# Masked token products of a chunked RWKV-7 mixer as 64x64 blocks on the array's quarters, and a pair's inversion ahead of the next pair's operands

## The chip, the core and the metric

One program on one core of a Trainium2 chip. The metric is the device time of one execution in microseconds; lower is better. The engines named below are TensorE (PE, whose weight loads are listed apart as PEld), VectorE (DVE), ScalarE (ACT), GpSimd (POOL) and SyncE (SP, which here only issues DMAs, in the order in which they stand in its queue). Each engine takes its instructions in program order and waits on semaphores.

## The reference, cut to what matters

One decoder layer on 512 tokens with a model width of 2048: a modulated RMS norm, one wide projection, two token mixers side by side (RWKV-7 and a gated width-3 convolution), a gated merge, an output projection and a residual. All arithmetic is fp32. The part that the change touches is the recurrence of the RWKV-7 mixer, 16 heads of size 64:

```
def step(S, inp):
    r_t, w_t, k_t, v_t, kk_t, b_t = inp
    sa = jnp.einsum('bhvk,bhk->bhv', S, -kk_t)
    S = (S * w_t[:, :, None, :] + sa[..., None] * b_t[:, :, None, :]
         + v_t[..., None] * k_t[:, :, None, :])
    y_t = jnp.einsum('bhvk,bhk->bhv', S, r_t)
    return S, y_t
```

## The kernel before

The recurrence is computed in chunks of C = 64 tokens, NC = 8 chunks, for a pair of heads at a time (two heads of 64 fill the 128 partitions), so there are NP = 8 pairs. In a chunk every product of one token's B or K row with another token's A or R row is needed (A is minus the normalised key, R the receptance, B and K the two things written to the state, each scaled by its decay). They are the tiles `GB` and `GK`, one 128 x 128 square per chunk: rows are the tokens of B (or K) of both heads, columns are the tokens of A and R.

The kernel has three stages. The first makes the normalised input as two fp32r halves (`hH`, `hL`) and opens some of the projection. The second, which the change is in, is `dense()`: 81 column tiles of the projection, each 48 matmuls of 128x128 weights and 512 moving columns (`ps_c`; half of each weight tile is split off by ACT and POOL as `wH_c` and `wL_c`), and between those matmuls the small work of the mixers. The third multiplies by the gates, `p_a`, `p_b` and `w_out`.

The order of the second stage on every engine is written by a planner in the kernel itself. Generators, the entries of the list `sides`, describe each piece of small work as steps with due times; `run(engine, cost, ...)` issues one instruction and books its cost on that engine, `take(tag, ...)` takes a PSUM bank when its last reader is due to be done, and `spend(t)` advances the clock `now` by PE's cost. At each step of the clock the entries of `sides` are asked in their order, and then one `dense()` matmul is issued. For each pair there are three of these pieces:

- `prepare` ("ops"): the operand tiles `AR` (A and R) and `BK` (B and K). In a square of `BK` each head stands in its own 64 partitions and its own 64 columns, and the other two quarters are zero; so the product of a square with `AR` over all 128 partitions keeps the heads apart.
- `invert` ("inv"): the products. For B and then for K, and for four chunks at a time, it takes one bank of tag `pg` (there are two), issues four fp32 matmuls 128x128 by 128 columns (L760), and lets DVE multiply the bank by a triangular 0/1 mask into `GG`. Then GB's 32x32 diagonal blocks go by DMA through DRAM (`s1`) into `M`, 31 steps of two DVE instructions (`invt`, `Xg`) invert them, copies and two more passes through DRAM (`s2`, `s3`) bring them to `XB` and `M`, and two sets of sixteen 32x32 matmuls (`pw`, `py`, L834) fill in the rest.
- `chunks`: transposes of BK and V, and then a chain over the eight chunks, in which PE, ACT and DVE take turns (`p1`, `p2`, `UB`, `SB`), group norm, and the transposes back by 64x64 matmuls on two of the array's quarters (tile `y`, L956).

An fp32 matmul leaves two records in the trace: `pg` has 128 matmuls and 256 records.

Of the kernel before, what the change touches and what calls it, by code (L numbers as in the profile page):

```python
# [8 lines left out]
F32 = mybir.dt.float32  # L9
F32R = mybir.dt.float32r  # L10
I32 = mybir.dt.int32
AF = mybir.ActivationFunctionType
ALU = mybir.AluOpType
# [3 lines left out]
P = 128  # L17
T = 512
# [4 lines left out]
NH = 2  # L23
HS = 64
C = 64
NC = T // C
HB = C // 2
# [8 lines left out]
HOP, SURE, SOON, SUM = 0.2, 0.6, 1.2, 0.35  # L36
# [40 lines left out]
def trunk(ctx: ExitStack, tc: tile.TileContext, xT_d, x_d, prm_d, adan_d, ada1_d, ada2_d, rows_d, w_d, lora_d, pa_d, pb_d,  # L77
          wo_d, out_d):
    nc = tc.nc
    V, A, G, TE, S = nc.vector, nc.scalar, nc.gpsimd, nc.tensor, nc.sync  # L80

    cst = ctx.enter_context(tc.tile_pool(name="cst", bufs=1))
# [9 lines left out]
    def bank(tag, name, n=T):  # L92

        return psp[tag].tile([P, T], F32, tag=tag, bufs=BANKS[tag], name=name)[:, 0:n]
# [21 lines left out]
    hsumr = cst.tile([P, P], F32R, name="hsumr")  # L116
    V.tensor_copy(hsumr, hsum)

    gmask = cst.tile([P, P], F32, name="gmask")
    G.memset(gmask, 1.0)  # L120
    for r0 in (0, C):
        for c0, op in ((r0, ALU.is_gt), (C - r0, ALU.is_ge)):
            G.affine_select(gmask[r0:r0 + C, c0:c0 + C], gmask[r0:r0 + C, c0:c0 + C], [[1, C]], op, 0.0, base=0,
                            channel_multiplier=-1)
    omu = cst.tile([P, 25], F32, name="omu")
    V.tensor_scalar(omu, pc("mu", 0, 25), -1.0, 1.0, ALU.mult, ALU.add)
    hw0 = cst.tile([P, 16], F32, name="hw0")
# [58 lines left out]
    with tc.tile_pool(name="ap", bufs=1) as ap, tc.tile_pool(name="psa", bufs=1, space=PSUM) as psa:  # L186
# [114 lines left out]
        for k in range(KT):  # L301
            g = 32 * (k % 4)
            TE.matmul(psc[g:g + 32, :], csb[:, k, :], adan[k // 8][:, k % 8, :], start=(k < 4), stop=(k >= KT - 4),
                      tile_position=(0, g))
# [29 lines left out]
        now = COST["begin"]  # L334
        clk = dict(dve=now + 1.4, act=now + 0.7, pool=now + 1.5, dma=now + 16.5)
        ready, lands, cut = {0: now}, {1: now + 2.0, 2: now + 9.8, 3: now + 16.5}, {b: now + 0.4 * b for b in range(3)}
# [5 lines left out]
        done, opened, units, at = 0, [], [], {}  # L342
# [63 lines left out]
        while units or opened:  # L406
# [3 lines left out]
            if u is None and units and len(opened) < NOPEN:  # L410
                b, t, k0, n = units[0]
# [8 lines left out]
            b, t, ps, k0, n, i = u  # L420
# [20 lines left out]
    with tc.tile_pool(name="rp", bufs=1) as rp, tc.manual_schedule(engines=ALL):  # L441


        now = 0.0
# [3 lines left out]
        def spend(t):  # L448
            nonlocal now
            now += t  # L450

        def run(eng, cost, f, *args, **kw):

            two = eng in ("POOL", "DVE2")
            e = eng[:3] if eng == "DVE2" else eng
            while busy[e] > now + SOON:
                yield busy[e] - SOON
            f(*args, **kw)  # L458
            t = max(now, busy[e])
            if two:  # L460
                while port and port[0][1] <= now:
                    port.pop(0)
                for b, c in port:
                    if b < t + cost and t < c:
                        t = c
                port.append((t, t + cost))
                port.sort()
            busy[e] = t + cost
            return busy[e] + HOP
# [9 lines left out]
        books = {tag: [[0.0] for _ in range(n)] for tag, n in BANKS.items()}  # L479

        def take(tag, name, n=T):
            while books[tag][0][0] is None or books[tag][0][0] > now:
                yield now + 0.25 if books[tag][0][0] is None else books[tag][0][0]
            books[tag].pop(0)
            book = [None]
            books[tag].append(book)
            return bank(tag, name, n), book

        def four(ps):
            return ps.rearrange("p (a b) -> p a b", a=4)  # L490
# [4 lines left out]
        def c3(t):  # L495
            return t.rearrange("p (c t) -> p c t", c=NC)
# [17 lines left out]
        halves = (slice(0, HS), slice(HS, P))  # L514


        hold, rkv, ops = {}, [dict() for _ in range(NP)], [dict() for _ in range(NP)]
# [141 lines left out]
        def prepare(j, got, out):  # L659
            n = f"_{j}"  # L660
# [3 lines left out]
            for i, b in enumerate(halves):  # L664
                o = halves[1 - i]
                t = yield from run("ACT", 0.3, A.activation, raw[o, 1, i].bitcast(F32R), raw[o, 0, i], AF.Copy)
# [3 lines left out]
                t = yield from run("POOL", 0.46, G.tensor_tensor, wa[o, i], raw[o, 0, i], raw[o, 1, i], ALU.subtract)  # L670
            yield t + SURE
            psw, book = yield from take("sm", "ps_w" + n)
# [5 lines left out]
            psa, book = yield from take("sm", "ps_a" + n)  # L678
            lowrank(psa, wa[:, 1], 1)
            yield from run("DVE", 0.55, V.tensor_scalar, lw, lw, -0.5 * DECAY, -0.5 * DECAY, ALU.mult, ALU.add)  # L680
            cum3 = c3(lw)
            for t0 in range(0, T, T // 4):
                t = yield from run("DVE2", 0.42, V.tensor_tensor_scan, lw[:, t0:t0 + T // 4],
                                   keep.rearrange("p c t -> p (c t)"), lw[:, t0:t0 + T // 4], 0.0, ALU.mult, ALU.add)
# [12 lines left out]
            kr = got["k"]  # L697
# [6 lines left out]
            psk, book = yield from take("sm", "ps_k" + n)  # L704
# [17 lines left out]
            AR = rp.tile([P, NC, P], F32, tag="AR", bufs=2, name="AR" + n)  # L722
            BK = BKs[j % 2]
            yield from run("DVE2", 0.7, V.tensor_tensor, a, kk, a, ALU.mult)
            for h, b in enumerate(halves):
                o = halves[1 - h]
                yield from run("DVE2", 0.7, V.scalar_tensor_tensor, AR[b, :, b], c3(kk)[b], -1.0, dec[b, :, 0:C], ALU.mult,
                               ALU.mult)
                yield from run("DVE2", 0.7, V.tensor_tensor, BK[b, :, 0, b], c3(a)[b], cum3[b], ALU.mult)
                yield from run("DVE2", 0.7, V.tensor_tensor, AR[b, :, o], c3(rr)[b], dec[b, :, 1:C + 1], ALU.mult)  # L730
                t = yield from run("DVE2", 0.7, V.tensor_tensor, BK[b, :, 1, b], c3(kr)[b], cum3[b], ALU.mult)

            u = yield from run("DVE2", 0.7, V.scalar_tensor_tensor, kr, rr, pc("rk", j), kr, ALU.mult, ALU.mult)
            out.update(AR=AR, end=end, vpad=got["vpad"], made=t)
# [7 lines left out]
            psb, book = yield from take("sm", "ps_b" + n)  # L742
# [6 lines left out]
        def invert(j, AR, out, made, **_):  # L749

            n = f"_{j}"
            yield made + SURE

            GB, GK = (yield from room_of("GG")) if j % 2 else (GG[:, 0], GG[:, 1])
            BK = BKs[j % 2]
            for i, g in enumerate((GB, GK)):
                for c0 in (0, 4):
                    pg, book = yield from take("pg", f"pg{n}_{c0}_{i}")
                    for k in range(4):
                        TE.matmul(four(pg)[:, k, :], BK[:, c0 + k, i, :], AR[:, c0 + k, :], start=True, stop=True)  # L760
                    spend(0.9)
                    yield now + SUM
                    book[0] = yield from run("DVE", 0.7, V.tensor_tensor, g[:, c0:c0 + 4, :], four(pg),
                                             gmask.unsqueeze(1).to_broadcast([P, 4, P]), ALU.mult)
                if not i:
                    ready = book[0]

            while at["z"] < j or not at["zeros"]:
                yield now + 0.3
# [52 lines left out]

            def lower(name, left, right, out):

                ps, books = [], []
                for h in range(NH):
                    p, book = yield from take("pg", f"{name}{h}{n}", NC * HB)
                    ps.append(p.rearrange("p (c t) -> p c t", c=NC))
                    books.append(book)
                for c in range(NC):  # L830
                    for h in range(NH):
                        l, r = left(h, c), right(h, c)
                        row = h * C + (HB if name == "py" else 0)
                        TE.matmul(ps[h][blk[h][1], c, :], l, r, start=True, stop=True,  # L834
                                  tile_position=(row, h * C + HB))
                spend(0.7)
                yield now + SUM
                for h in range(NH):
                    t = yield from run("ACT", 0.38, A.activation, out(h), ps[h][blk[h][1]], AF.Copy)
                    books[h][0] = t  # L840
                return t

            yield SURE + (yield from lower("pw", lambda h, c: GB[blk[h][0], c, blk[h][1]],
# [5 lines left out]
        def chunks(j, AR, GB, GK, bon, end, vpad, solved, **_):  # L849

            n = f"_{j}"
# [4 lines left out]
            BK = BKs[j % 2]  # L856
# [17 lines left out]
            for c0, m in ((0, 4), (4, 4), (8, 1)):  # L874
                pv, book = yield from take("pg", f"pv{n}_{c0}")
                pv = four(pv)
                for k in range(m):
                    TE.transpose(pv[:, k, :], vpad[:, (c0 + k) * C:(c0 + k + 2) * C], ident)
                spend(0.11 * m)
                yield now + SUM  # L880
                for h, b in enumerate(halves):

                    k0, k1 = max(c0 + h - 1, 0), min(c0 + m + h - 1, NC)
                    if k0 < k1:
                        w0 = k0 + 1 - h - c0
                        t = yield from run("ACT", 0.38, A.activation, VB[b, k0:k1, b], pv[b, w0:w0 + k1 - k0, b], AF.Copy)
                book[0] = t
            turned.add(j)
            yield max(turned_b, solved) + SURE
# [199 lines left out]
        def side(name, behind, make):  # L1089
            for j in range(NP):  # L1090
                while not behind(j):
                    yield now + 0.3
                yield from make(j)
                at[name] = j + 1
# [8 lines left out]
        for i in range(NFULL):  # L1103
# [2 lines left out]
        sides = [[g, 0.0] for g in (  # L1106
            high(), low(), loader(), uses(soon), uses(due),
            side("chunks", lambda j: "solved" in ops[j] and "bon" in ops[j], lambda j: chunks(j, **ops[j])),
            side("ops", paced, lambda j: prepare(j, rkv[j], ops[j])),
            side("inv", lambda j: at["made"] > j, lambda j: invert(j, out=ops[j], **ops[j])),  # L1110
            zeros())]
        stream, idle = dense(), 0.0
        while stream or any(sd[0] for sd in sides[5:]) or due or soon:
# [298 lines left out]
```

## Time and profile before

| what | value |
|---|---|
| median of 3 runs | 1621.15 us (1621.15 to 1621.32) |
| the profiled execution: time, span of its core | 1618.96 us, 1617.0 us |
| mean granted TensorE clock | 0.996 |
| PE, DVE, POOL, ACT busy | 99%, 58%, 50%, 40% of the span |
| stage 2 | about 188 to 1236 us |
| first `pg` matmul of the first and of the last pair | 261.7 us and 1047.0 us |
| DMA | 235.72 MB, mean 146 GB/s |

PE's busy time counts the whole way of a matmul through the array, and matmuls overlap, so what one of them costs is read as the distance from its start to the next start and not as its duration (`ps_c` lasts 396 ns in the trace, and the starts are nearer together). Idle time of the other engines costs nothing as long as PE has no wait for them.

### The profile page before, as it was taken

To read this page: it belongs to the slowest core of one execution; us is meant where nothing else is said; L and a number is where in the kernel's file an instruction comes from. 1 tells how busy PE (TensorE), PEld (TensorE's weight loads), DVE (VectorE), ACT (ScalarE), POOL (GpSimd) and SP (SyncE) were. 2 spreads that over 40 slices of the span, in tenths; PEclk is the share of its full clock that TensorE was granted. 3 is DMA by queue.
4 is the path that set the end of the run, shared out by engine and by line. 5 is a ranking of instruction groups with operands and counts; after the bars stand their busy time and mean duration, and the time that the engine had idled before them with its cause. 6 is when DMAs were issued, how large, how long until landed. Compare 5 with 4: busy or idle time off the path is not lost.

```text
span 1617.0 us, 23221 instructions
## 1 busy us (share of the span) xinstructions
PE 1593.0 (99%) x8194; PEld 1323.1 (82%) x8194; DVE 931.4 (58%) x1643; ACT 641.2 (40%) x1305; POOL 812.7 (50%) x648
## 2 busy tenths in 40 slices
PE   7999999999999999999999999999999999999997
PEld 6788878888888888888888888888888888888886
DVE  6997397764978827816869359353111354453404
ACT  5554442324545235335443353344433223223421
POOL 2799574553435534544445435434344446765421
PEclk9999999999999999999999999999999999999999
DMA  9986334333322343333333433434353786765714
GB/s 365 366 333 212 102 117 112 97 111 87 101 85 85 100 118 88 102 112 106 96 99 99 115 105 94 127 101 116 92 166 117 242 266 192 202 206 171 240 36 150
DMA packets 139172, 235.72 MB, mean 146 GB/s; under 512 B 34864, under 2 KB 43696, under 8 KB 135216
## 3 DMA queue, kind: packets, MB, share of 16 engines
q1 hardware_dynamic: 138912, 234.15, 47.0%
q8 instruction: 65, 1.06, 0.3%
q14 instruction: 51, 0.42, 0.1%
q10 hardware_dynamic: 144, 0.09, 0.0%
HBM read 214.78 MB, written 19.14 MB: 145 GB/s over the span
## 4 chain that ended last, share of the span: by engine, by line
PE 95%; DVE 3%; ACT 1%; issue 0%; DMA 0%; POOL 0%; POOLq 0%; ACTq 0%
PE ps_c L1071 53%; PE fps L162 3%; PE fps L161 3%; PE fps L160 3%; PE po L161 3%; PE po L160 3%; PE po L162 3%; PE py_a L162 2%; PE py_b L161 2%; PE py_a L160 2%; PE py_b L160 2%; PE py_b L162 2%; PE py_a L161 2%; PE pg L760 2%; PE pl L162 1%; PE pl L161 1%
## 5 line engine op out<-in xcount | busy, mean ns | idle before, releaser
L458 POOL TENSOR_TENSOR wL_c<-raw_c,wH_c 128x512 fp32r<-128x512 f32 x324 | 440.9, 1362 | 538.2 <-ACT wH_c L458 508.4
L1071 PE MATMUL ps_c<-hH,wL_c 128*128 128x512 f32 x1296 | 513.3, 396 | 0.7 <-POOL wL_c L458 0.7
L1071 PE MATMUL ps_c<-hH,wH_c 128*128 128x512 f32 x1296 | 513.6, 396 | 0.0
L1071 PE MATMUL ps_c<-hL,wH_c 128*128 128x512 f32 x1296 | 512.0, 395 | 0.0
L458 ACT ACTIVATE wH_c<-raw_c 128x512 fp32r<-128x512 f32 x324 | 204.1, 630 | 423.7 <-PE ps_c L1071 270.0
L1071 PEld LDWEIGHTS ps_c<-hH,wL_c 128*128 128x128 f32 x1296 | 243.8, 188 | 48.6 <-POOL wL_c L458 1.1
L1071 PEld LDWEIGHTS ps_c<-hL,wH_c 128*128 128x128 f32 x1296 | 243.8, 188 | 47.0
L1071 PEld LDWEIGHTS ps_c<-hH,wH_c 128*128 128x128 f32 x1296 | 243.8, 188 | 46.8
L149 POOL TENSOR_TENSOR fL<-fraw,fH 128x512 fp32r<-128x512 f32 x56 | 79.8, 1434 | 45.6 <-ACT fH L148 45.4
L458 DVE TENSOR_TENSOR Xg<-Xg,invt 128x60 f32<-128x60 f32 (+24 forms) x248 | 92.3, 372 | 7.9
L149 POOL TENSOR_TENSOR oL<-wo,oH 128x512 fp32r<-128x512 f32 x48 | 65.8, 1379 | 61.0 <-ACT oH L148 58.3
L160 PE MATMUL fps<-hH,fH 128*128 128x512 f32 x224 | 88.8, 396 | 3.5 <-ACT hH L269 3.5
L458 DVE TENSOR_TENSOR invt<-M,Xg 128x60 f32<-128x60 f32 (+24 forms) x248 | 87.1, 351 | 7.9
L161 PE MATMUL fps<-hL,fH 128*128 128x512 f32 x224 | 88.8, 396 | 2.2 <-DVE hL L272 2.2
L162 PE MATMUL fps<-hH,fL 128*128 128x512 f32 x224 | 88.5, 395 | 1.7 <-POOL fL L149 1.7
L458 DVE TENSOR_TENSOR GG<-pg,gmask 128x512 f32<-128x512 f32 x32 | 22.1, 691 | 108.5 <-PE pg L760 108.5
L161 PE MATMUL po<-oL,mH 128*128 128x512 f32 x192 | 74.8, 390 | 0.0
L160 PE MATMUL po<-oH,mH 128*128 128x512 f32 x192 | 74.7, 389 | 0.0
L162 PE MATMUL po<-oH,mL 128*128 128x512 f32 x192 | 74.7, 389 | 0.0
L254 DVE SCALAR_TENSOR_TENSOR ada<-ada,csr 128x2048 f32<-128x2048 f32 x30 | 68.1, 2275 | 0.0
L148 ACT ACTIVATE oH<-wo 128x512 fp32r<-128x512 f32 x64 | 38.3, 627 | 74.8 <-PE po L162 47.8
L149 POOL TENSOR_TENSOR wL_pb<-raw_pb,wH_pb 128x512 fp32r<-128x512 f32 x32 | 42.2, 1318 | 45.3 <-ACT wH_pb L148 45.3
(285 smaller groups left out, 2597.3 us busy)
## 6 DMA issues: line engine op xcount, KB each, us to landing
raw_c<-in_w_dram SPq DMA_DIRECT2D x324, 256.0 KB, 2.7
ada<-in_ada_dram SPq DMA_DIRECT2D x30, 1024.0 KB, 8.7
gr<-in_ada_dram SPq DMA_DIRECT2D x64, 256.0 KB, 4.6
wo<-in_wo_dram SPq DMA_DIRECT2D x64, 256.0 KB, 3.8
fraw<-in_w_dram SPq DMA_DIRECT2D x56, 256.0 KB, 4.6
raw_pb<-in_pb_dram SPq DMA_DIRECT2D x32, 256.0 KB, 2.8
raw_pa<-in_pa_dram SPq DMA_DIRECT2D x32, 256.0 KB, 3.0
th_s<-th SPq DMA_DIRECT2D x30, 256.0 KB, 2.0
```

The lines of the kernel that those rows point to most:

```text
L148: A.activation(H, src, AF.Copy)
L149: eng.tensor_tensor(L, src, H.bitcast(F32), ALU.subtract)
L160: TE.matmul(ps, wH, xH, start=start, stop=False)
L161: TE.matmul(ps, wH, xL, start=False, stop=False)
L162: TE.matmul(ps, wL, xH, start=False, stop=stop)
L254: V.scalar_tensor_tensor(ada[j, i], ada[j, i], 1.0, csr, ALU.mult, ALU.mult, accum_out=accs[j][:, i:i + 1])
L458: f(*args, **kw)
L760: TE.matmul(four(pg)[:, k, :], BK[:, c0 + k, i, :], AR[:, c0 + k, :], start=True, stop=True)
L1071: TE.matmul(ps, w[:, i, :], x[k], start=(k == k0 and x is hH and w is H), stop=(k == KT - 1 and w is L))
```

## The change

Three things change, with the same sums computed.

First, a block of products for four chunks is no longer four 128x128 matmuls with half of the weights zero, once for B and once for K. It is sixteen 64x64 matmuls: for each chunk, B of each head and K of each head, each on a quarter of the array (`tile_position`), with 128 moving columns as before. So that the four quarters are all different, K's tokens stand with the second head first: `BK[b, :, 1, o]` in place of `BK[b, :, 1, b]`. The result of B goes to one bank and that of K to the other, so that both banks are taken at once (`take_both`). V's tokens (`VB`) are put in the same order as K's, and the mask becomes three column blocks, of which B uses the first two and K the last two. `lower` takes its two banks with `take_both` too.

Second, `take` waits while `take_both` is collecting its banks. The planner's charge for four chunks of B and K goes from 2 x 0.9 to 1.44.

Third, in `sides` the entry "inv" stands ahead of "ops".

```
-    gmask = cst.tile([P, P], F32, name="gmask")
+    gmask = cst.tile([P, 3 * C], F32, name="gmask")
     G.memset(gmask, 1.0)
...
+    for i, r0 in enumerate((0, C)):
+        for c in range(3):
+            g = gmask[r0:r0 + C, c * C:(c + 1) * C]
+            G.affine_select(g, g, [[1, C]], ALU.is_ge if (c + i) % 2 else ALU.is_gt, 0.0, base=0, channel_multiplier=-1)
...
         def take(tag, name, n=T):
-            while books[tag][0][0] is None or books[tag][0][0] > now:
-                yield now + 0.25 if books[tag][0][0] is None else books[tag][0][0]
+            while tag in pairs or books[tag][0][0] is None or books[tag][0][0] > now:
+                yield now + 0.25 if tag in pairs or books[tag][0][0] is None else books[tag][0][0]
...
+        def take_both(tag, name, n=T):
+            while tag in pairs:
+                yield now + 0.25
+            pairs.add(tag)
+            for b in books[tag][:]:
+                while b[0] is None or b[0] > now:
+                    yield now + 0.25 if b[0] is None else b[0]
+            pairs.remove(tag)
+            books[tag] = [[None], [None]]
+            return [bank(tag, f"{name}_{i}", n) for i in range(2)], books[tag][:]
...
-                t = yield from run("DVE2", 0.7, V.tensor_tensor, BK[b, :, 1, b], c3(kr)[b], cum3[b], ALU.mult)
+                t = yield from run("DVE2", 0.7, V.tensor_tensor, BK[b, :, 1, o], c3(kr)[b], cum3[b], ALU.mult)
...
-            for i, g in enumerate((GB, GK)):
-                for c0 in (0, 4):
-                    pg, book = yield from take("pg", f"pg{n}_{c0}_{i}")
-                    for k in range(4):
-                        TE.matmul(four(pg)[:, k, :], BK[:, c0 + k, i, :], AR[:, c0 + k, :], start=True, stop=True)
-                    spend(0.9)
-                    yield now + SUM
-                    book[0] = yield from run("DVE", 0.7, V.tensor_tensor, g[:, c0:c0 + 4, :], four(pg),
-                                             gmask.unsqueeze(1).to_broadcast([P, 4, P]), ALU.mult)
-                if not i:
-                    ready = book[0]
+            for c0 in (0, 4):
+                ps, pair = yield from take_both("pg", f"pg{n}_{c0}")
+                ps = [four(p) for p in ps]
+                for k in range(4):
+                    for i in range(2):
+                        for h, b in enumerate(halves):
+                            o = halves[h ^ i]
+                            TE.matmul(ps[i][o, k, :], BK[b, c0 + k, i, o], AR[b, c0 + k, :], start=True, stop=True,
+                                      tile_position=(b.start, o.start))
+                spend(1.44)
+                yield now + SUM
+                for i, g in enumerate((GB, GK)):
+                    pair[i][0] = yield from run("DVE", 0.7, V.tensor_tensor, g[:, c0:c0 + 4, :], ps[i],
+                                                 gmask[:, i * C:i * C + P].unsqueeze(1).to_broadcast([P, 4, P]), ALU.mult)
+                ready = pair[0][0]
...
-                        t = yield from run("ACT", 0.38, A.activation, VB[b, k0:k1, b], pv[b, w0:w0 + k1 - k0, b], AF.Copy)
+                        t = yield from run("ACT", 0.38, A.activation, VB[b, k0:k1, o], pv[b, w0:w0 + k1 - k0, o], AF.Copy)
...
             side("chunks", lambda j: "solved" in ops[j] and "bon" in ops[j], lambda j: chunks(j, **ops[j])),
+            side("inv", lambda j: at["made"] > j, lambda j: invert(j, out=ops[j], **ops[j])),
             side("ops", paced, lambda j: prepare(j, rkv[j], ops[j])),
-            side("inv", lambda j: at["made"] > j, lambda j: invert(j, out=ops[j], **ops[j])),
```

What this does to the order on PE is seen at the products of pair 3 (`pg_3_0` are its chunks 0 to 3, the last digit is 0 for B and 1 for K, `ps_c` is the dense stream). In the kernel before, B's four chunks are one piece of four matmuls, and K's for the same chunks come some dense matmuls later, each beside a transpose of the pair before:

```order
L1071 MATMUL ps_c56_5497<-hL13_1409,wH_c56_3_5499 128x512
L864 MATMUL pt_2_0_0_5611<-ident_77,BK0_1802 128x128 x4
L760 MATMUL pg_3_0_0_5616<-AR_3_5201,BK1_3059 128x128 x4
L1071 MATMUL ps_c56_5497<-hH13_1408,wL_c56_3_5517 128x512
L1071 MATMUL ps_c56_5497<-hH14_1480,wH_c56_3_5499 128x512
```

After the change, B and K of the same chunks alternate in one piece of sixteen matmuls:

```order
L1089 MATMUL ps_c48_5584<-hH2_488,wH_c48_0_5510 128x512
L1089 MATMUL ps_c48_5584<-hL2_489,wH_c48_0_5510 128x512
L1089 MATMUL ps_c48_5584<-hH2_488,wL_c48_0_5517 128x512
L779 MATMUL pg_3_0_0_5612<-AR_3_5474,BK1_3292 64x128 x2
L779 MATMUL pg_3_0_1_5613<-AR_3_5474,BK1_3292 64x128 x2
```

The last two rows stand there four times, once for each chunk. There are two such pieces per pair, where there were four of four matmuls.

On DVE the place is the end of pair 3's inversion (`invt_3`, `Xg_3`), where the operands of pair 4 (`sq_4`, `kk_4`, `ku_4`) and the group norm of pair 2 (`st_2`) stand. Before, the inversion is interrupted two steps from its end, and 43 rows of other work follow before its step 29:

```order
L458 TENSOR_TENSOR invt_3_28_6204<-M_3_5764,Xg_3_5765 128x24
L458 TENSOR_TENSOR Xg_3_5765<-Xg_3_5765,invt_3_28_6204 128x24
L458 TENSOR_SCALAR sq_4_6151<-ps_k_4_6200 128x512
L458 TENSOR_SCALAR kk_4_6218<-sq_4_6151 128x512
L458 TENSOR_SCALAR kk_4_6218<-kk_4_6218 128x512
L458 TENSOR_TENSOR ku_4_6221<-kk_4_6218 128x512
```

After the change it runs to its end and the copies follow at once:

```order
L459 TENSOR_TENSOR invt_3_28_6180<-M_3_5705,Xg_3_5706 128x24
L459 TENSOR_TENSOR Xg_3_5706<-Xg_3_5706,invt_3_28_6180 128x24
L459 TENSOR_TENSOR invt_3_29_6198<-M_3_5705,Xg_3_5706 128x16
L459 TENSOR_TENSOR Xg_3_5706<-Xg_3_5706,invt_3_29_6198 128x16
L459 TENSOR_TENSOR invt_3_30_6207<-M_3_5705,Xg_3_5706 128x8
L459 TENSOR_TENSOR Xg_3_5706<-Xg_3_5706,invt_3_30_6207 128x8
L459 COPY M_3_5705<-Xg_3_5706 32x256 x4
```

Counted over all pairs, the other DVE instructions between a pair's first and last inversion step were 40, 19, 67, 70, 16, 63, 65 and 8 for pairs 0 to 7, and are 3, 27, 28, 28, 25, 28, 23 and 22. On PE the dense matmuls that stand between a pair's first `pg` and its first `pw` were 422, 237, 437, 448, 225, 402, 433 and 210, and are 231, 296, 282, 275, 284, 262, 241 and 243. The last pair's first `pt` has 3458 of the stage's 3888 dense matmuls ahead of it before, and 3147 after.

More of the change, by code (lines that the diff above doesn't have):

```diff
@@ L117, in trunk @@
     V.tensor_copy(hsumr, hsum)
-    gmask = cst.tile([P, P], F32, name="gmask")
+    gmask = cst.tile([P, 3 * C], F32, name="gmask")
     G.memset(gmask, 1.0)
[L121 to L124, printed above, removed]
+    for i, r0 in enumerate((0, C)):
+        for c in range(3):
+            g = gmask[r0:r0 + C, c * C:(c + 1) * C]
+            G.affine_select(g, g, [[1, C]], ALU.is_ge if (c + i) % 2 else ALU.is_gt, 0.0, base=0, channel_multiplier=-1)
     omu = cst.tile([P, 25], F32, name="omu")
@@ L487, in take @@
             return bank(tag, name, n), book
+        pairs = set()
+        def take_both(tag, name, n=T):
[8 more added lines that the diff above has]
+            return [bank(tag, f"{name}_{i}", n) for i in range(2)], books[tag][:]
         def four(ps):
@@ L823, in lower @@
             def lower(name, left, right, out):
[L825 to L829, printed above, removed]
+                ps, pair = yield from take_both("pg", f"{name}{n}", NC * HB)
+                ps = [p.rearrange("p (c t) -> p c t", c=NC) for p in ps]
                 for c in range(NC):
@@ L839, in lower @@
                     t = yield from run("ACT", 0.38, A.activation, out(h), ps[h][blk[h][1]], AF.Copy)
-                    books[h][0] = t
+                    pair[h][0] = t
                 return t
@@ L883, in chunks @@
                     k0, k1 = max(c0 + h - 1, 0), min(c0 + m + h - 1, NC)
+                    o = halves[1 - h]
                     if k0 < k1:
                         w0 = k0 + 1 - h - c0
-                        t = yield from run("ACT", 0.38, A.activation, VB[b, k0:k1, b], pv[b, w0:w0 + k1 - k0, b], AF.Copy)
+                        t = yield from run("ACT", 0.38, A.activation, VB[b, k0:k1, o], pv[b, w0:w0 + k1 - k0, o], AF.Copy)
                 book[0] = t
```

## The prediction

> **What bounds the kernel now.** I read the page first, then the windows over the second stage, in which all of the change lies.
>
> ```profile
> span 1617.0 us, 23221 instructions
> PE 1593.0 (99%) x8194; PEld 1323.1 (82%) x8194; DVE 931.4 (58%) x1643; ACT 641.2 (40%) x1305; POOL 812.7 (50%) x648
> PE 95%; DVE 3%; ACT 1%; issue 0%; DMA 0%; POOL 0%; POOLq 0%; ACTq 0%
> core 0: us, PE busy (x) PEld busy (x) DVE busy (x) ACT busy (x) POOL busy (x), PEclk, DMA share, GB/s
> 188.00:1236.00 1048.00, 1045.61 (x5785) 873.06 (x5785) 633.77 (x1255) 434.05 (x921) 494.35 (x402) 1.00 0.37 106
> ```
>
> The third row is the chain that ended last: 95% of it is PE. In the last row PE stands still for 2.4 of the stage's 1048 us, with its clock granted in full, while DVE is busy for 60% of it and ACT and POOL for less than half. So the stage is as long as PE's list is, and what is taken from that list shortens the run by as much, as long as nothing comes too late for PE. The next two views are the instructions on tile `pg` and PE's timeline around the first of them (start, duration).
>
> ```profile
> L760 PE MATMUL pg<-AR,BK x256: 270/275/276, 261.7 to 1056.4; 128*128 128x128 f32 x128
>   DVE GG L458: 108.5, 32
> 259.68 0.39 PE L1071 MATMUL ps_c<-hL,wH_c 128*128 128x512 f32 x1
> 261.50 0.39 PE L1071 MATMUL ps_c<-hH,wH_c 128*128 128x512 f32 x1
> 261.73 1.05 PE L760 MATMUL pg<-AR,BK 128*128 128x128 f32 x8
> 262.53 0.48 PE L1071 MATMUL ps_c<-hL,wH_c 128*128 128x512 f32 x1
> 262.85 0.40 PE L1071 MATMUL ps_c<-hH,wL_c 128*128 128x512 f32 x1
> 263.08 1.05 PE L760 MATMUL pg<-AR,BK 128*128 128x128 f32 x8
> ```
>
> A dense matmul costs (261.50 - 259.68)/8 = 0.2275 us, start to start. From one `pg` piece to the next are 263.08 - 261.73 = 1.35 us with two dense matmuls inside, so a piece of four fp32 matmuls (eight records) costs 1.35 - 0.455 = 0.895 us, or 0.112 us per record of 128 columns. There are 32 pieces: 28.6 us of PE. The row under the first says that DVE waits for `pg` and not the other way round.
>
> **The products on quarters.** A piece of sixteen 64x64 matmuls takes the place of two such pieces, which cost 2 x 0.895 = 1.79 us. It has 32 records, each again with 128 columns. All hangs on how many of them run at a time. Three places of the kernel before use parts of the array. Two are on PE's timeline, the inversion's 32x32 matmuls and the 64x64 transposes back, each of sixteen matmuls (32 records) that alternate between two parts which share neither rows nor columns of the array:
>
> ```profile
> 363.12 0.39 PE L1071 MATMUL ps_c<-hH,wL_c 128*128 128x512 f32 x1
> 363.44 0.69 PE L834 MATMUL pw<-XB,GG 32*32 32x32 f32 x32
> 364.40 0.40 PE L1071 MATMUL ps_c<-hL,wH_c 128*128 128x512 f32 x1
> 444.81 0.40 PE L1071 MATMUL ps_c<-hH,wH_c 128*128 128x512 f32 x1
> 445.14 1.15 PE L956 MATMUL y<-ident,VY 64*64 64x64 f32 x32
> 446.56 0.40 PE L1071 MATMUL ps_c<-hH,wL_c 128*128 128x512 f32 x1
> ```
>
> Between the two dense starts of each triple lie two dense steps and the piece. `pw` costs 364.40 - 363.12 - 0.455 = 0.825 us, `y` 446.56 - 444.81 - 0.455 = 1.295 us. The same count with 32 more columns each costs 0.47 us more. If two records run at a time there are 16 rounds, and a round grows by 0.0294 us for 32 columns, or 0.918 ns per column. That is near the 0.112/128 = 0.874 ns which one full-size record costs per column, so two parts do run together, at almost full rate each. What is left, 0.825 - 16 x 32 x 0.918 ns = 0.355 us, is fixed: getting into the small form and out of it. The third place, in the chain of waits of the first stage, says what four parts do:
>
> ```profile
> 6.08 7.19 PE csr L247 x32
> 18.49 3.44 PE psc L303 x32
> L247 PE MATMUL csr<-csT,ident x32: 416/416/577, 6.1 to 12.9; 16*128 16x128 f32 x32
> L303 PE MATMUL psc<-adan,csb x32: 504/632/634, 18.4 to 21.4; 128*32 128x256 f32 x32
> ```
>
> `csr` has all 128 columns of the array in use: 7.19/32 = 0.225 us for 128 moving columns, 1.755 ns per column. That is twice `pg`'s 0.874, so PE ran at half its rate there. `psc` goes round four parts of 32 columns each, with 256 moving columns: 3.44/32 = 0.1075 us, 0.420 ns per column, 4.2 times as fast as `csr` beside it. So four parts that share all their rows run four at a time. Not shown is a pair of parts that share their columns and lie in different rows, as B of one head and K of the other do now, and four parts at PE's full rate.
>
> I take four at a time, since that is what `psc` did: 8 rounds of 128 columns at 0.918 ns are 0.940 us, with the fixed 0.355 us 1.295 us per piece. It saves 1.79 - 1.295 = 0.495 us, and with two pieces in each of 8 pairs **7.9 us**. Its bounds: at `pg`'s 0.874 ns and with half of the fixed part belonging to the 16 rounds of `pw` and not to the change of form, the piece is 0.895 + 0.18 = 1.07 us and the saving 11.5 us. From the other side, with two at a time 16 rounds of 0.112 and 0.355 make 2.15 us, a loss of 5.7 us; with none together 32 x 0.112 + 0.355 = 3.94 us, a loss of 34 us. I stay near the low end, since `psc` has the same count of parts and only their place differs.
>
> **The other edits** cost nothing on PE. K's tokens second head first is another address in the same DVE instruction; VB's copies and the wider mask the same; two more `affine_select` lie at the start on POOL. DVE's 32 products with the mask stay 32 of the same size; they now come two in a row after both banks. If that cover went, one more of them would stand before the DMAs of `s1`, 0.69 us by this row:
>
> ```profile
> L458 DVE TENSOR_TENSOR GG<-pg,gmask x32: 690/691/693, 262.8 to 1056.7; 128x512 f32<-128x512 f32 x32
> ```
>
> **The inversion ahead of the operands** moves no work on or off PE; it changes what may come late. A pair's way from `pg` to `pw` is now 231 to 296 dense matmuls long and holds 3 to 28 other DVE instructions. `pw` waits for `XB`'s DMA; behind `pw` the whole dense stream would stand, and behind a late `s2` or `XB` on SP the loads of the dense weights (`raw_c`). Before, pair 7 already ran nearly so, with 210 dense matmuls and 8 other instructions:
>
> ```profile
> L458 DVE TENSOR_TENSOR invt<-M,Xg x31: 166/217/1281, 1068.4 to 1095.0; 128x60 f32<-128x60 f32 x3, 128x28 f32<-128x28 f32 x2, 128x54 f32<-128x54 f32 x2, 128x48 f32<-128x48 f32 x2
> L473 SPq DMA_DIRECT2D XB<-s x4: 315/442/448, 1104.1 to 1105.5; - x4
> DMA to landing us min/median/max: 1.8/1.9/1.9
> 1109.85 0.69 PE L834 MATMUL pw<-XB,GG 32*32 32x32 f32 x32
> ```
>
> The last block was due at 1105.5 + 1.9 = 1107.4 and PE came to it at 1109.85: 2.4 us to spare, with the shortest way of all. The ways after the change are 21 to 86 dense matmuls longer (5 to 20 us), against up to 20 more DVE instructions, most of them the group norm's small ones. So I book no wait. The stage's end is safe too: the last pair moves up by 311 dense matmuls, 71 us at 0.2275.
>
> **Sum.** Profiled execution: 1618.96 - 7.9 = 1611.1 us, its span 1617.0 - 7.9 = 1609.1. The median of the runs is 2.2 us above the profiled one; from it, 1621.15 - 7.9 = **1613.2 us**.
>
> **The rivals.**
>
> *Less than four at a time, but some gain.* The planner's own charge for a piece, 1.44 where two pieces were charged 1.8, would save 0.36 x 16 = 5.8 us: 1615.4. A charge is no measurement, but the old charge of 0.9 for four matmuls agrees with the 0.895 above. Against it: `psc`.
>
> *Two at a time: slower.* A product's two records are passes over the same part of the array. If matmuls start strictly in the order in which they are issued, a second pass holds up the next part's first, and only neighbours overlap. The piece is then 2.15 us, and the time 1621.15 + 5.7 = 1626.9. It decides from where a round of four costs more than (1.79 - 0.355)/8 = 0.179 us. `pw` and `y` fit it as well as they fit my reading, since two parts are all they have; `psc` does not, since by it its 32 records would have taken twice the 3.44 us. The Trainium skill has this rule ("TensorE: Matmul & The Clock Gate", Part 3: matmuls are strict first-in first-out in start and end, and weight loads overlap a running matmul only in another row group). By that rule the time would be the 1626.9 just named; the row of `psc`, whose parts share their rows, does not agree with it.
>
> *The inversion comes late.* If the way of every pair is 3 us short of what DVE and the passes through DRAM need, PE waits 8 x 3 = 24 us: 1637. It eats the gain from a mean of 1 us per pair, a slip of 3.4 us against pair 7 of before. For it: single inversion instructions reached 1281 ns where the median is 217. Against it: that pair 7 had the same long ones and was in time.
>
> *It doesn't do what it says.* If the order of the rounds were lost between the pieces, or new waits of 0.5 us at the 16 pieces ate the gain, the time would stay at 1621.
>
> **How the numbers follow.** My forecast 0.62 (1609.5 to 1615), the smaller gain 0.17, two at a time 0.09, the late inversion 0.07, no effect 0.05. The point is the forecast's, 1613.2. For the range, the lower end takes the bound of 11.5 us as far as 1609.5; the upper end takes in the smaller gain and waits of 3 us with it, 1615.4 + 3 = 1618.5; outside lie the two slower rivals and no effect. A measurement of this kernel tells about 0.2%, 3.2 us, from no change: faster is below 1617.9. Faster has the forecast, most of the smaller gain and a little of a late inversion by less than 1 us: 0.80. Same 0.10, slower 0.10.
>
> **What would show it.** `pg` from its first start to the second dense start behind it, less the dense steps: 1.25 to 1.3 us per piece if I am right, 1.44 or 2.15 by the rivals, and its records in eight rounds of four starts. The stage's end near 1228 in place of 1236, with PE's idle time in it still 2 to 4 us. A late inversion would show as idle time of PE ended by the DMA of `XB` or of `raw_c`, on `pw` or `ps_c`. I am wrong if the sum of `pg` falls by less than 6 us, or if it falls and the stage's end does not.

## The result and the profile after

The changed kernel takes 1610.83 us (median of 6 runs, 1609.13 to 1612.08) against 1621.15 us (median of 6 runs) before: a ratio of 0.9938 with a 95% interval from 0.9927 to 0.9948, or 8.4 to 11.8 us less. The forecast was 1613.2 us, 7.9 us less, in a range from 1609.5 to 1618.5. The profiled execution took 1612.08 us, its span is 1610.1 us.

The rows of the changed kernel's page that answer to those shown of before, the span and the busy times:

```profile
span 1610.1 us, 23745 instructions
PE 1585.3 (98%) x8450; PEld 1308.9 (81%) x8450; DVE 926.0 (58%) x1643; ACT 640.5 (40%) x1305; POOL 804.9 (50%) x650
```

The windows view of the changed kernel over the second stage:

```profile
core 0: us, PE busy (x) PEld busy (x) DVE busy (x) ACT busy (x) POOL busy (x), PEclk, DMA share, GB/s
190.00:1229.00 1039.00, 1036.90 (x6045) 858.12 (x6044) 626.71 (x1255) 434.01 (x922) 486.41 (x402) 1.00 0.38 107
```

PE has 256 records more and is busy for less time. The second stage is 1039 us long where it was 1048, and PE stands still for 2.1 us of it, as it did for 2.4 before. In this execution the stage begins 2 us later than in the one shown of before, with the first stage's list unchanged but for two small POOL instructions at 3 us; that part of the difference between the two executions is taken as not the change's. The run of the new order alone, which has the first stage of before, begins its second stage at 189.8 us, and the run quarter by quarter, with the two POOL instructions, at 188.5 us.

The changed kernel's instructions on tile `pg` (shortest, median and longest in ns, then the starts of the first and the last in us):

```profile
L779 PE MATMUL pg<-AR,BK x512: 269/269/321, 264.3 to 982.6; 64*64 64x128 f32 x171
```

And PE's timeline around the first piece (start, duration in us):

```profile
263.95 0.39 PE L1089 MATMUL ps_c<-hH,wH_c 128*128 128x512 f32 x1
264.27 1.10 PE L779 MATMUL pg<-AR,BK 64*64 64x128 f32 x32
265.31 0.50 PE L1089 MATMUL ps_c<-hL,wH_c 128*128 128x512 f32 x1
265.65 0.40 PE L1089 MATMUL ps_c<-hH,wL_c 128*128 128x512 f32 x1
```

From the dense start before the piece to the second one behind it are 265.65 - 263.95 = 1.70 us; less two dense steps of 0.2275 us the piece costs 1.245 us, where the two pieces that it replaces cost 1.79. That is 0.545 us for each of 16, 8.7 us in all. The last `pg` stands at 982.6 us where it stood at 1056.4.

The rounds can be counted. In these windows over the same piece, the (x) behind PE's busy time says how many of its 32 records had started by the end of the window:

```profile
core 0: us, PE busy (x) PEld busy (x) DVE busy (x), PEclk, DMA share, GB/s
264.26:264.42 0.16, 0.15 (x4) 0.15 (x8) 0.00 (x0) 1.00 0.00 0
264.26:264.46 0.20, 0.19 (x8) 0.19 (x12) 0.00 (x0) 1.00 0.00 0
264.26:265.08 0.82, 0.81 (x28) 0.81 (x32) 0.00 (x0) 1.00 0.00 0
264.26:265.12 0.86, 0.85 (x32) 0.85 (x32) 0.00 (x0) 1.00 0.00 0
```

Four records start within 0.020 us, the second four 0.160 us after the first, and the eighth four at 0.815 us. So there are eight rounds of four, (0.815 - 0.160)/6 = 0.109 us apart.

### The profile page after: what moved, and what is told of

It is laid out like the page before. It is cut to its first block, busy times and chain, and to the rows that moved or that the text cites. A ratio compares the mean times of both kernels' runs of the same rounds, so it can differ in the third digit from the quotient of the medians.

```text
span 1610.1 us, 23745 instructions
## 1 busy us (share of the span) xinstructions
PE 1585.3 (98%) x8450; PEld 1308.9 (81%) x8450; DVE 926.0 (58%) x1643; ACT 640.5 (40%) x1305; POOL 804.9 (50%) x650
## 4 chain that ended last, share of the span: by engine, by line
PE 91%; DVE 4%; POOL 2%; issue 1%; DMA 1%; ACT 1%; POOLq 0%; SPq 0%; DVEq 0%; ACTq 0%
PE ps_c L1089 52%; PE fps L162 3%; PE fps L163 3%; PE fps L161 3%; PE po L162 2%; PE po L163 2%; PE po L161 2%; PE py_b L162 2%; PE py_b L161 2%; PE py_b L163 2%; PE py_a L163 1%; PE py_a L162 1%; PE py_a L161 1%; PE pg L779 1%; PE pl L162 1%
## 5 line engine op out<-in xcount | busy, mean ns | idle before, releaser
L459 POOL TENSOR_TENSOR wL_c<-raw_c,wH_c 128x512 fp32r<-128x512 f32 x324 | 434.3, 1341 | 534.9 <-ACT wH_c L459 526.9
L459 DVE TENSOR_TENSOR invt<-M,Xg 128x60 f32<-128x60 f32 (+24 forms) x248 | 91.4, 368 | 9.7 <-DMA M<-s 1.8
L150 DVE TENSOR_TENSOR bL<-yb,bH 128x512 fp32r<-128x512 f32 x8 | 7.3, 981 | 121.9 <-ACT bH L149 121.9
L459 DVE SCALAR_TENSOR_TENSOR SB<-p,end,SB 64x64 f32<-64x64 f32 x96 | 27.2, 283 | 81.8 <-PE p L938 73.6
```

What stands on the lines that cost most here:

```text
L150: eng.tensor_tensor(L, src, H.bitcast(F32), ALU.subtract)
```

## The experiments

All ratios are to the kernel before, from runs on the same chip. The experiments were run in two groups, in which the kernel before took 1620.45 us (quarters with the old order, new order alone, two quarters, quarter by quarter) and 1620.9 us (the other four), beside 1621.15 with the change; so a difference between medians of different groups is uncertain by about 0.7 us.

| kernel | median us | ratio | 95% interval |
|---|---|---|---|
| the change | 1610.83 | 0.9938 | 0.9927 to 0.9948 |
| quarters, old order of the entries | 1620.5 | 1.0003 | 0.9994 to 1.0012 |
| new order alone | 1619.39 | 0.9993 | 0.9984 to 1.0002 |
| both banks at once alone | 1629.21 | 1.005 | 1.0038 to 1.0063 |
| the change, two quarters | 1624.29 | 1.0022 | 1.0012 to 1.0031 |
| the change, quarter by quarter | 1633.51 | 1.0081 | 1.0067 to 1.0095 |
| the change, one piece per pair | 1618.52 | 0.9985 | 0.9977 to 0.9994 |
| quarters, old order, one more gate tile | 1617.23 | 0.9977 | 0.9969 to 0.9986 |
| the change, one more gate tile | 1617.07 | 0.9975 | 0.9965 to 0.9985 |

**The products on quarters, with the old order of the entries.**

```
             side("chunks", ...),
-            side("inv", ...),
             side("ops", ...),
+            side("inv", ...),
```

> The changed kernel with the entry for a pair's inversion put back behind the entry for the next operands; the products stay on quarters. The theory: the gain is PE time of the 16 pieces, 1.79 - 1.24 = 0.55 us each, 8.8 us, and the order of the two entries is worth at most the few waits of PE (2.4 us idle in the stage before): 1611 to 1613 us. The rival, that a good part of the 10.3 us came from the order: 1614 us or more.

1620.5 us: nothing is left of the gain. The rival's "1614 us or more" holds the number, but not as it was meant: the new order brings nothing by itself, as the next run shows. The second stage has kept its gain, and the loss stands behind it. The windows over the stage and over the 25 us after its last dense matmul:

```profile
core 0: us, PE busy (x) PEld busy (x) DVE busy (x) ACT busy (x) POOL busy (x), PEclk, DMA share, GB/s
189.00:1226.50 1037.50, 1035.91 (x6010) 855.98 (x6009) 640.64 (x1235) 433.37 (x918) 495.64 (x401) 1.00 0.37 105
1226.50:1251.50 25.00, 18.67 (x95) 14.23 (x94) 14.03 (x29) 10.80 (x19) 7.67 (x6) 0.86 0.42 136
```

In the changed kernel PE has no idle time in the same place, and its clock is whole:

```profile
core 0: us, PE busy (x) PEld busy (x) DVE busy (x) ACT busy (x) POOL busy (x), PEclk, DMA share, GB/s
1229.00:1253.00 24.00, 24.00 (x108) 19.87 (x107) 8.68 (x10) 10.48 (x19) 12.46 (x9) 1.00 0.50 149
```

Here PE stands still for 6.3 us of the 25, and the granted clock is 0.86, which costs 0.14 x 25 = 3.5 us more. With the last pair's `y`, 1.3 us of PE work that now lies in the third stage, that is 11.1 us. The stage before it is 1.5 us shorter than in the changed kernel (1037.5 against 1039), which leaves 9.6; the medians differ by 9.7. What is late is seen in the rows of tile `y`, of the kernel before, of the changed kernel and of this one:

```profile
L956 PE MATMUL y<-ident,VY x256: 218/218/267, 445.1 to 1181.7; 64*64 64x64 f32 x128
```

```profile
L974 PE MATMUL y<-ident,VY x256: 218/218/267, 395.1 to 1104.0; 64*64 64x64 f32 x128
```

```profile
L974 PE MATMUL y<-ident,VY x256: 218/218/267, 447.2 to 1234.8; 64*64 64x64 f32 x128
```

This kernel's PE timeline there, with the waits in brackets:

```profile
1233.92 1.15 PE L974 MATMUL y<-ident,VY 64*64 64x64 f32 x32 [1.60 <-DVE VY L459]
1245.03 0.79 PE L161 MATMUL py_b<-bH,wH_pb 128*128 128x512 f32 x1 [4.53 <-ACT wH_pb L149]
```

The last pair's transposes back came at 1181.7 us before, come at 1104.0 after the change, and at 1234.8 here, 8 us behind the last dense matmul. PE waits 1.6 us for them, and later 4.5 us for the first operands of `py_b`, the third stage's product with `p_b`. The chain of waits names the link between the two:

```profile
1235.97 1.31 POOL y L459
1237.30 0.70 DVE za L459
1238.02 0.33 SPq L1187
1239.34 4.46 DMA yb<-yb_s
1243.83 0.63 ACT bH L149
```

The third stage loads the `yb` that it waits for only when the last pair's `za` is done at 1238.00, and the one of this row lands at 1243.8; ACT makes `bH` of it and right behind it the `wH_pb` that PE's row names. So by this chain the loss hangs on when the last pair ends. What made it late is the subject of the third run.

**The new order alone**, with the 128x128 products of before.

```
             side("chunks", ...),
+            side("inv", ...),
             side("ops", ...),
-            side("inv", ...),
```

> The kernel before with the entry for a pair's inversion ahead of that for the next operands and nothing else; the products stay 128x128. The theory: PE's list is the same, so the time stays within 1619 to 1622 us. The rival, that the order gave part of the gain: 1616 to 1619 us.

1619.39 us; the interval of the ratio, 0.9984 to 1.0002, holds no change. At most 2.6 us come from the order by itself. It does bring the pairs forward: the last pair's transposes back come at 1076.2 us, where they came at 1181.7 before. But before they were in time already, with 239 of the dense matmuls behind them. Neither part alone brings anything that can be told from nothing, and together they bring 10.3 us.

**Both banks at once alone.** The kernel before, with its 128x128 products and its old order. Beside the lines below it takes `take_both`, `take`'s wait while both banks are collected, and `take_both` in `lower`:

```
-            for i, g in enumerate((GB, GK)):
-                for c0 in (0, 4):
-                    pg, book = yield from take("pg", f"pg{n}_{c0}_{i}")
-                    for k in range(4):
-                        TE.matmul(four(pg)[:, k, :], BK[:, c0 + k, i, :], AR[:, c0 + k, :], start=True, stop=True)
-                    spend(0.9)
+            for c0 in (0, 4):
+                ps, pair = yield from take_both("pg", f"pg{n}_{c0}")
+                ps = [four(p) for p in ps]
+                for k in range(4):
+                    for i in range(2):
+                        TE.matmul(ps[i][:, k, :], BK[:, c0 + k, i, :], AR[:, c0 + k, :], start=True, stop=True)
+                spend(1.8)
...
```

> The kernel before, its products 128x128, with one thing of the change: B and K of the same four chunks in one piece that takes both banks at once (and the two banks of the 32x32 products too), the inversion still behind the next operands. If the late last pair (its transposes back with none of the 3888 dense matmuls behind them, 239 before) comes from taking both banks, this kernel loses at the stage's end what the quarters alone lost there, 381 to 393 us from the last dense matmul to the end: 1620.5 + 11 = about 1631 us. If the quarters themselves were the cause of that end: 1620 us.

1629.21 us, 8 us slower than before, with no quarter in it. The loss has the same place and form as in the first run, by the rows of tile `y` and by the windows over the stage and the 25 us behind its last dense matmul:

```profile
L968 PE MATMUL y<-ident,VY x256: 217/218/268, 448.8 to 1242.7; 64*64 64x64 f32 x128
```

```profile
core 0: us, PE busy (x) PEld busy (x) DVE busy (x) ACT busy (x) POOL busy (x), PEclk, DMA share, GB/s
188.00:1234.40 1046.40, 1044.61 (x5754) 872.78 (x5753) 641.55 (x1235) 432.84 (x918) 494.73 (x401) 1.00 0.37 104
1234.40:1259.40 25.00, 17.98 (x98) 13.77 (x97) 14.02 (x29) 10.81 (x19) 7.13 (x6) 0.93 0.42 131
```

So it is the taking of both banks, which the quarters need, that leaves the last pair late while the next operands stand ahead of the inversion. Which of its parts does it (B and K in one piece, `take`'s wait, `lower`) was not separated. On PE the first products of pairs 2 to 7 come 117 to 132 us apart in the first run (503.6, 635.8, 753.2, 870.5, 987.8 and 1105.2 us), and 102 to 106 us apart in the changed kernel (467.7, 574.1, 677.7, 780.0, 882.4, 978.2 us; 96 for the last). Before they came 102 to 125 us apart, and with the new order alone 96 to 101. So both banks hold the pairs back and the new order brings them forward. Why the planner spaces them so is not shown.

**One more gate tile in the second stage**, to give the late pair dense matmuls to stand behind, and the same for the changed kernel as a control.

```
-NGB, NGA = 16, 14
+NGB, NGA = 16, 15
```

> The products on quarters with the inversion behind the next operands, as in the first run, and one more gate tile (48 dense matmuls, 10.9 us of PE) done in the second stage and not in the third: 12 dense matmuls now stand behind the last transposes back. If the gain of the quarters was lost because the last pair ended after the dense stream, part of the 11.4 us in the stage's tail comes back: 1610 to 1617 us, less than the 1620.5 without it. If it was lost elsewhere, the time stays at 1620 us.

> The control for the run before: the changed kernel with the same gate tile done in the second stage. Its last pair is in time already, so the move should give nothing: 1610 to 1612 us.

With the old order the time falls from 1620.5 to 1617.23 us, a little short of the expected range. In the 25 us behind the last dense matmul, where the first run lost its time, PE no longer stands still, and its clock is whole (columns as in the windows above):

```profile
1240.70:1265.70 25.00, 25.00 (x112) 20.73 (x111) 9.04 (x13) 11.58 (x21) 12.26 (x9) 1.00 0.69 227
```

The control was a miss: 1617.07 us and not 1610 to 1612, so the tile's move has a price of its own, about 6 us. It is in the third stage, where PE waits for the halves of `ya` once, and then runs for a while at a lower clock. PE's timeline of the control, and the window around it:

```profile
1346.25 0.80 PE L161 MATMUL py_a<-aH,wH_pa 128*128 128x512 f32 x1 [3.88 <-ACT aH L149]
```

```profile
core 0: us, PE busy (x) PEld busy (x) DVE busy (x) ACT busy (x) POOL busy (x), PEclk, DMA share, GB/s
1337.00:1362.00 25.00, 21.11 (x82) 16.94 (x81) 11.16 (x16) 7.14 (x12) 11.37 (x10) 0.86 0.65 189
```

The run with the old order pays it too, with a wait of 4.1 us at the same place. So beside that control it says what it was made for: with dense matmuls behind the last pair the old order and the new take the same time, 1617.2 and 1617.1 us. Without them they differ by 9.7 us. What the order is worth lies at the end of the stage.

**Two quarters in place of four.** K's tokens are not swapped, so B and K of a head go to one quarter on the diagonal; V and the mask follow.

```
-                t = ... V.tensor_tensor, BK[b, :, 1, o], c3(kr)[b], cum3[b], ALU.mult)
+                t = ... V.tensor_tensor, BK[b, :, 1, b], c3(kr)[b], cum3[b], ALU.mult)
...
-                            o = halves[h ^ i]
+                            o = b
...
```

> The changed kernel with K's tokens (and V's, and the mask) not swapped, so that B and K of a head go to the same quarter and only the two quarters on the diagonal are in use; the count of matmuls is the same. The theory, that a round is as many records as there are different quarters: 16 rounds of 0.109 us and the fixed 0.37 make 2.11 us per piece, 0.87 more than with four, 14 us in 16 pieces: about 1625 us. The rival, that only neighbouring matmuls overlap and four different quarters are not what counts: no change, 1611 us.

1624.29 us, as expected. PE's timeline around the first piece:

```profile
263.51 0.39 PE L1089 MATMUL ps_c<-hH,wH_c 128*128 128x512 f32 x1
263.82 1.96 PE L779 MATMUL pg<-AR,BK 64*64 64x128 f32 x32
266.06 0.40 PE L1089 MATMUL ps_c<-hH,wL_c 128*128 128x512 f32 x1
```

The piece costs 2.55 - 0.455 = 2.095 us, 0.85 more for the same 32 records: 16 rounds in place of 8, by this difference 0.106 us for a round and by the starts in the trace 0.109, as in the changed kernel. With two quarters the products on parts of the array would have been slower than the 128x128 ones (2.095 against 1.79). The fixed part of a piece, which does not grow with its rounds, is 1.245 - 8 x 0.109 = 0.373 us.

**Quarter by quarter.** The same sixteen matmuls in another order.

```
-                for k in range(4):
-                    for i in range(2):
-                        for h, b in enumerate(halves):
+                for i in range(2):
+                    for h, b in enumerate(halves):
+                        for k in range(4):
                             o = halves[h ^ i]
```

> The changed kernel with the sixteen matmuls of a piece issued quarter by quarter (four chunks of one quarter, then the next) and no longer one quarter after the other. If PE looks ahead over the whole piece, the rounds of four stay and the time is 1611 us. If it looks ahead over a few records only, as the alternation of before needed, the quarters run nearly one after the other: 32 records of 0.109 us less what overlaps at three borders, some 3.5 us per piece, 2.3 more than now, 36 us in all: about 1647 us.

1633.51 us, between the two expectations.

```profile
262.19 0.39 PE L1089 MATMUL ps_c<-hH,wH_c 128*128 128x512 f32 x1
262.50 2.56 PE L779 MATMUL pg<-AR,BK 64*64 64x128 f32 x32
265.34 0.40 PE L1089 MATMUL ps_c<-hH,wL_c 128*128 128x512 f32 x1
```

The piece costs 3.15 - 0.455 = 2.695 us. Less the fixed 0.373 that is 2.322/0.109 = 21.3 rounds for 32 records: some ten are saved at three borders, about three at each. The first border is seen in the count of started records (columns as in the windows over the changed kernel's first piece):

```profile
262.50:262.98 0.48, 0.47 (x4) 0.48 (x5) 0.00 (x0) 1.00 0.00 0
262.50:263.02 0.52, 0.52 (x6) 0.52 (x7) 0.00 (x0) 1.00 0.00 0
```

Four records start one by one; then the fifth and the sixth start within 0.006 us. That is too near for one quarter, whose records start 0.109 us apart, so the sixth is taken for the next quarter's first, started while three of the first quarter's eight were left. The starts of the rest of the piece fit the same count at the other two borders. So PE does not pick freely from the piece, but it isn't strictly in order either: that each engine takes its instructions in program order, as it is said at the start, does not hold for these starts.

**One piece per pair**, to save half of the ways into the small form and out of it: the second four chunks take the two banks of tag `pc` and follow at once.

```
-            for c0 in (0, 4):
-                ps, pair = yield from take_both("pg", f"pg{n}_{c0}")
+            for tag, c0 in (("pg", 0), ("pc", 4)):
+                ps, pair = yield from take_both(tag, f"pg{n}_{c0}")
...
-                spend(1.44)
+            spend(2.11)
```

> The changed kernel with both pieces of a pair in one: the second piece takes its two banks from tag pc, which the chain over the chunks uses, and its matmuls follow the first piece's at once. Theory, that 0.37 us of each piece is the way into the small form and out of it: 8 of 16 such ways go, 2.9 us: about 1608 us. Rival, that the chain waits for its banks of tag pc and the pairs end later: 1611 us or more.

1618.52 us: the rival held in its figure. For the piece itself the theory held:

```profile
262.23 0.39 PE L1092 MATMUL ps_c<-hH,wH_c 128*128 128x512 f32 x1
262.55 1.98 PE L780 MATMUL pg<-AR,BK 64*64 64x128 f32 x64
264.80 0.40 PE L1092 MATMUL ps_c<-hH,wL_c 128*128 128x512 f32 x1
```

It costs 2.57 - 0.455 = 2.115 us, where two pieces cost 2.49. The 0.375 us saved is the fixed part once, 3.0 us in 8 pairs. More is lost elsewhere. The windows view of the second stage, and the timeline of DVE and PE at the first of the places where PE now waits:

```profile
core 0: us, PE busy (x) PEld busy (x) DVE busy (x) ACT busy (x) POOL busy (x), PEclk, DMA share, GB/s
188.70:1235.80 1047.10, 1038.43 (x6041) 862.05 (x6040) 605.40 (x1255) 434.13 (x921) 486.38 (x402) 1.00 0.37 106
```

```profile
496.77 1.78 DVE L459 TENSOR_TENSOR VY<-VY,st 128x512 f32<-128x512 f32 x1
498.69 1.15 PE L977 MATMUL y<-ident,VY 64*64 64x64 f32 x32 [1.84 <-DVE invt L459]
500.45 0.63 PE L1092 MATMUL ps_c<-hH,wL_c 128*128 128x512 f32 x1
```

PE stands still for 8.7 us of the stage, 6.6 more than in the changed kernel, nearly all of it in three waits in front of `y` (1.84, 2.42 and 2.22 us). Behind each of the three the trace's clock records give half the clock for 3.4 us, another 1.7 us lost each time. `y` needs a bank of tag `pc` as well, but the bank is not what holds it: in all three places PE starts `y` 0.14 to 0.15 us after DVE has ended the last write of `VY`, the tile that `y` reads (here 496.77 + 1.78 = 498.55 and 498.69). So it is DVE that is late there, with the group norm of the pair; why, the runs do not show. The rival's reason, the banks and the end of the pairs, is not what is seen: the pairs ended in time. This is no better kernel, and the changed one remains the fastest that was run.

## Why the prediction was right, and where it wasn't

- **The bound.** Right: the stage is as long as PE's list, its idle time went from 2.4 to 2.1 us, and the products' 8.7 us came off the time.
- **Four at a time.** Right, and shown: the piece takes 8 rounds, with two quarters 16. Two things that the trace of before did not show held as well, quarters that share their columns, and PE's full rate. The step to it from `psc` was weaker than it was put. That PE ran at half its rate there was read off `csr` alone: the windows view gives a granted clock of 1.00 for 6.00 to 13.30 us, and the trace's clock records begin only at 21.7 us, so by the clock it is not shown. At the full 0.874 ns per column the 0.420 of `psc` would be two at a time.
- **The size.** The term "1.295 us per piece" was too high by 0.05 us, 0.8 us in 16 pieces. The rate per column was the error: 0.918 ns came from the difference of `y` and `pw`, and a round of four costs 0.109 us, 0.85 ns per column, below even `pg`'s 0.874 as I read it. The fixed part was nearly right, 0.355 against 0.373. Of the measured 10.3 us, 8.7 are the pieces. The new order's own 1.1 us (between -0.3 and 2.6) may be the rest, which stays unproven.
- **"The other edits cost nothing on PE."** This step failed. Taking both banks at once by itself costs 8 us, at the end of the stage and not in the pieces. I had named the banks only as a matter of where DVE's two products with the mask stand.
- **"The stage's end is safe too."** True of the change as it was; PE's list of waits has none for `XB`, and for the last pair the last `XB` block was issued at 1036.0 us and landed 1.8 us later, and PE came to `pw` at 1042.4, 4.6 us to spare. But what the inversion ahead of the operands is worth was misjudged. I compared the change with the kernel before, where the last pair had 239 dense matmuls behind it, and not with the quarters in the old order, where it had none. The order, which I booked at nothing, holds off 9.7 us.
- **The rivals.** Two at a time did not happen, and its price was right: 2.15 us per piece against the 2.095 measured with two quarters. The planner's 1.44 was too high for a piece of 1.245. The late inversion did not come.
- So the forecast was right for its main term, and right in its total by luck: of the two edits booked at nothing, one costs 8 us by itself and the other gives 9.7 back once the first is made. They cancelled without my having weighed either.

## What to carry to other kernels

When a change needs a resource in a new way (here two PSUM banks at once), ask what that alone does to the order of the work, as a step with its own price, and look at the last piece of work behind which a stage has nothing to hide. Two edits that each measure as nothing can be worth ten microseconds together, so undo them one at a time before one is called harmless. For matmuls on parts of the array, count the rounds: records over different parts that follow each other, plus a fixed part for each piece.

## What the runs showed of the hardware that I had not expected

- Four 64x64 quarters run at once for fp32 at a granted clock of 1.00, 0.109 us for four records of 128 columns each, also where two share their rows and two their columns; one full-size record takes 0.112. A piece on quarters has a fixed part of about 0.37 us, which is paid once per piece: one piece of 64 records costs 2.115 us where two of 32 cost 2.49.
- How matmuls of different quarters are interleaved in the program decides: 1.245 us per piece one after the other, 2.695 us quarter by quarter, with the same instructions. The Trainium skill calls matmuls strictly first-in first-out ("TensorE: Matmul & The Clock Gate", Part 3). By that rule the changed kernel's piece would have cost the two-at-a-time price of 2.15 us; its 1.245 does not agree.
- A wait of PE can cost more than itself. After 4.5 us of waiting at 1245 us in the first run the granted clock of the 25 us around it is 0.86, 3.5 us more. In the kernel with one piece per pair a wait of 1.84 us was followed by dense matmuls that last 0.63 us where they last 0.39. The first run's wait of 1.60 us at 1233.9 was not: the matmuls behind it last 0.39 to 0.40 again. From which length on it happens these runs do not show.
